# The first inner tile of two up projections computed by plain products, with the pair sums of the late token tile behind it

## The chip, the cores and the metric

The kernel runs on 1 core of one Trainium2 chip. The metric is the device time of a run in microseconds (us): the median of 3 runs before the change is 2680.4 us (2679.09 to 2680.55).

## What is computed

One inference step of a decoder trunk of two layers: an S5 layer with a GLU, a ConvFFN, the projection to keys and values, attention, and a second ConvFFN. It handles 1024 prompt tokens and 64 sample tokens of width 1024. The change touches the up projection of the ConvFFN (`w_up` is 1024 x 5632, gate and val with 2816 columns each), which runs once in each layer:

```
def conv_ffn(x, buf, w_up, conv_w, conv_b, w_down):
    seq_len = x.shape[1]
    h = x @ w_up
    hp = jnp.concatenate([buf.astype(h.dtype), h], axis=1)
    hc = conv_b + conv_w[0] * hp[:, 0:seq_len]
    for tap in range(1, CONV_W):
        hc = hc + conv_w[tap] * hp[:, tap:tap + seq_len]
    gate, val = jnp.split(hc, 2, axis=-1)
    out = (jax.nn.gelu(gate) * val) @ w_down
    return out, hp[:, -(CONV_W - 1):]

x = x + rmsnorm(a_out, post_g)                       # the layer's mixer or attention
x = x + rmsnorm(conv_ffn(rmsnorm(x, f_pre_g), ...))  # twice: layer 0 and layer 1
```

## The kernel before

**Three products for one.** Every operand is split into a high part in the matmul's format and a low part with the rest (`split_evac`: ACT casts the high part in line 144, DVE subtracts for the low part in line 145). A product is three matmuls, hi·hi, lo·hi and hi·lo (`mm3`, lines 809 to 811).

**Tokens.** The normed tokens stand transposed in `xT_hi` and `xT_lo`, 128 to a tile: prompt tiles 0 to 7 and the 64 sample tokens (NTT). The matrix product before (GLU output in layer 0, `o_proj` in layer 1) ends token tile by token tile in the order NTT, 0, 3, 1, 4, 2, 5, 6, 7; the first five are called EARLY. Each goes through a queue (`Tail`): square sum on ACT (824), post norm and residual sum on DVE (854), square sum, second norm on DVE (864), then at `pop` the transposes on PE (870) and the split into `xT`. What stands last in the queue when the up projection begins is popped between its first products.

**Seven products for eight.** An inner tile f is 128 gate and 128 val columns, 22 tiles in all. For the first 768 tokens the kernel does not form the 8 block products (2 halves of the inner axis 1024, 2 token groups of 384, gate and val) but 7, in the manner of Strassen and Winograd. That needs sums on both sides. On the token side `Combos.pair` (905 to 919) is called for token tiles 3, 4 and 5, each paired with 0, 1, 2: t1 = yb_a - ya_a (911), t3 (912), t2 (913), t4 (914), a and b being the halves of a token row. t1 and yb_b go into `xT`, t2 to t4 into 8 tiles of their own. On the weight side `inputs(f)` loads the raw gate and val tiles (512 KB each, two buffers), forms s1 to s4 on DVE (1109 to 1112, 128x512 each) and splits 4 weight tiles of 128x1024 (whi on ACT, wlo on DVE). `first(f)` runs the 7 products, 12 matmuls of 384 columns each, 84 in all; `rest(f, s)` runs 24 matmuls of 320 columns for the other tokens; `conv` and `outputs` follow on ACT, DVE and POOL and end in a store to the scratch tensor `gd`, from which the down projection loads its pieces (gr<-gd).

**The start.** Tile 0 runs its first product and copies it (1146), then pops token 5 with its pair sums, then 6, then 7, then the rest.

**What sets the order.** The program text gives the dependences; a scheduler with a model of the timeline lays out each engine's queue, so that an edit at one place can change the order elsewhere. Each engine, and SP, which issues the DMAs, works its queue in order.

Of the kernel before, what the change touches and what calls it, by code (L numbers as in the profile page):

```python
# [12 lines left out]
F32R = mybir.dt.float32r  # L13
I32 = mybir.dt.int32
AF = mybir.ActivationFunctionType
ALU = mybir.AluOpType
# [21 lines left out]
NF = FF // P  # L38
# [35 lines left out]
def trunk_kernel(ctx, tc, I, O):  # L74
    nc = tc.nc
    V = nc.vector
    A = nc.scalar
# [4 lines left out]
    def nm(s):  # L82
        uid[0] += 1
        return f"{s}_{uid[0]}"
# [6 lines left out]
    def psum(tag="mm"):  # L91
        return pspool.tile([P, 512], F32, tag=tag, name=nm(tag), bufs=5 if tag == "mm" else 3)
# [48 lines left out]
    def split_evac(hi_ap, lo_ap, ps_ap, scale=None):  # L141

        if scale is None:
            A.copy(hi_ap, ps_ap)  # L144
            V.tensor_tensor(lo_ap, ps_ap, hi_ap.bitcast(F32), ALU.subtract)  # L145
        else:
            A.mul(hi_ap, ps_ap, scale)
            V.scalar_tensor_tensor(lo_ap, ps_ap, scale, hi_ap.bitcast(F32), op0=ALU.mult, op1=ALU.subtract)
# [608 lines left out]
    EARLY, LATE = ORDER_O[:5], ORDER_O[5:]  # L757
# [108 lines left out]
    def transposed(y, n):  # L866
        ps = psum_t()
        m = y.shape[1] // P
        for c in range(m):
            PE.transpose(ps[:, c * n : (c + 1) * n], y[:, c * P : (c + 1) * P], ident[0:n, 0:n])  # L870
        return ps[:, 0 : m * n].rearrange("p (c t) -> p c t", c=m)

    def tail_b(y, tt, scale=None):

        t0, n = tokens(tt)
        for h in range(2):
            split_evac(xh[:, 4 * h : 4 * h + 4, t0 : t0 + n], xl[:, 4 * h : 4 * h + 4, t0 : t0 + n],
                       transposed(y[:, 512 * h : 512 * h + 512], n), scale)
# [4 lines left out]
    HT = 384  # L883

    class Combos:
        def __init__(self):
            self.tiles = [slot("acc", [P, 3, HT], F32R) for _ in range(8)]
# [5 lines left out]
        def rhs(self, s, kt):  # L893

            return [self.view(s, part, kt)[:, 0] for part in range(2)]
# [8 lines left out]

        def pair(self, ya, yb, tt):

            t0 = tt * P
            tr = lambda y: transposed(y, P)
            t1, t2, t3, t4 = [slot("gr") for _ in range(4)]
            a, b = slice(0, 512), slice(512, D)  # L910
            V.tensor_tensor(t1, yb[:, a], ya[:, a], ALU.subtract)
            V.tensor_tensor(t3, yb[:, b], yb[:, a], ALU.subtract)
            V.tensor_tensor(t2, yb[:, b], t1, ALU.subtract)
            V.tensor_tensor(t4, ya[:, b], t2, ALU.subtract)
            split_evac(xh[:, 0:4, t0 : t0 + P], xl[:, 0:4, t0 : t0 + P], tr(t1))
            split_evac(xh[:, 4:8, t0 : t0 + P], xl[:, 4:8, t0 : t0 + P], tr(yb[:, b]))
            for s, t in enumerate((t2, t3, t4)):
                self.store(s, tr(t), t0 - HT)

    class Tail:  # L920
# [1 line left out]


        def __init__(self):
            self.n, self.q, self.combos, self.gain, self.lag = [], [], None, None, 2

        def add(self, y, tt, *a, aside=False, **kw):
            tail_a(y, tt, *a, aside=aside, **kw)
# [11 lines left out]
        def pop(self):  # L940
            if self.q:
                y, tt = self.q.pop(0)
                if self.combos and HT <= tt * P < 2 * HT:
                    self.combos.pair(self.first, y, tt)
                else:
                    tail_b(y, tt)
                    self.first = y

    tail = Tail()

# [139 lines left out]
    def ffn_up(i, down):  # L1090
# [3 lines left out]
        u3 = lambda t: t.rearrange("p (k f) -> p k f", f=P)  # L1094

        st, cvos = {}, {}
        cb = tail.combos

        def inputs(f):
            raws, hbs = [], []  # L1100
            for s in range(2):
                raw = pools["w"].tile([P, 1024], F32, tag="raw", name=nm("raw"), bufs=2)
                rv = u3(raw)
                nc.sync.dma_start(rv, wv[:, :, s * FF + f * P : s * FF + (f + 1) * P])
                raws.append(rv)
            a11, a12, a21, a22 = [r[:, 4 * k : 4 * k + 4] for r in raws for k in range(2)]
            s12, s34 = u3(slot("xr")), u3(slot("xr"))
            s1, s2, s3, s4 = [t[:, 4 * k : 4 * k + 4] for t in (s12, s34) for k in range(2)]
            V.tensor_tensor(s1, a21, a22, ALU.add)
            V.tensor_tensor(s2, s1, a11, ALU.subtract)  # L1110
            V.tensor_tensor(s3, a11, a21, ALU.subtract)
            V.tensor_tensor(s4, a12, s2, ALU.subtract)
            ws = []
            for r in (raws[0], s12, s34, raws[1]):
                hi, lo = u3(wslot("whi", F32R)), u3(wslot("wlo", F32R))
                split_evac(hi, lo, r)
                ws.append((hi, lo))
# [17 lines left out]
        NAHEAD = 1  # L1135

        def first(f):


            (wg, w12, w34, wv_), (hg, hv), _ = st[f]  # L1140
            lo, hi = slice(2, 2 + HT), slice(2 + HT, 2 + 2 * HT)
            p1, p2, p3 = psum(), psum(), psum()
            v1, v2, v3 = [t[:, 0:HT] for t in (p1, p2, p3)]
            m1, u2, u3_ = hv[:, lo], hg[:, hi], hv[:, hi]
            prod(p1, wg, 0, x(0, 0), True)
            A.copy(m1, v1)  # L1146
            if f < NAHEAD:
                prod(p1, wg, 4, x(4, 0), False)
                A.copy(hg[:, lo], v1)
                yield  # L1150
# [6 lines left out]
            if f >= NAHEAD:  # L1157
                prod(p1, wg, 4, x(4, 0), False)
                A.copy(hg[:, lo], v1)
# [58 lines left out]


        inputs(0)  # L1220
        g = first(0)
        for _ in range(3):
            next(g)
            tail.pop()
        while tail.q:
            tail.pop()
        for s in range(2):
            rest(0, s)
            conv(0, s)
        outputs(0)  # L1230
        for f in range(NAHEAD, NF):
# [819 lines left out]
    first = {}  # L2051
# [52 lines left out]
```

## Time and profile before

| | us |
|---|---|
| median of 3 runs | 2680.4 |
| the profiled run's own time | 2684.83 |
| its span, first to last instruction | 2682.9 |
| PE busy / DVE busy / ACT busy in the span | 2500.6 / 1963.5 / 1270.9 |
| the up projection of layer 0 begins | 436.2 |
| the up projection of layer 1 begins | 1908 |

The mean granted clock of PE is 0.976. PE is TensorE, DVE is VectorE, ACT is ScalarE, POOL is GpSimd; PEld are PE's weight loads. A timeline line gives the start, the length, the engine, the line of the kernel, the operation, out<-in, the shape, and in brackets how long the engine had been idle and what ended it. Matmul records are longer than their pitch, since they overlap; the distance between two starts is what one costs.

### The profile page before, as it was taken

To read this page: it belongs to the slowest core of one execution; us is meant where nothing else is said; L and a number is where in the kernel's file an instruction comes from. 1 tells how busy PE (TensorE), PEld (TensorE's weight loads), DVE (VectorE), ACT (ScalarE), POOL (GpSimd) and SP (SyncE) were. 2 spreads that over 40 slices of the span, in tenths; PEclk is the share of its full clock that TensorE was granted. 3 is DMA by queue.
4 is the path that set the end of the run, shared out by engine and by line. 5 is a ranking of instruction groups with operands and counts; after the bars stand their busy time and mean duration, and the time that the engine had idled before them with its cause. 6 is when DMAs were issued, how large, how long until landed. Compare 5 with 4: busy or idle time off the path is not lost.

```text
span 2682.9 us, 39622 instructions
## 1 busy us (share of the span) xinstructions
PE 2500.6 (93%) x14234; PEld 2203.5 (82%) x14234; DVE 1963.5 (73%) x3683; ACT 1270.9 (47%) x2559; POOL 657.3 (24%) x1062
## 2 busy tenths in 40 slices
PE   3778998999999989999999899989799999998997
PEld 2777887999999967778777788877699999996775
DVE  7994358777777789984232688875877777778999
ACT  6763334444444454354322677764544444444432
POOL 3220030111111175501201222113011111137661
PEclk9999998999999999999999899999899999999998
DMA  5443233222222233444646433335322222233334
GB/s 145 99 98 88 85 124 124 65 83 74 74 74 74 89 116 92 127 145 166 204 157 211 104 79 95 97 105 171 115 69 79 74 74 74 74 104 107 94 102 145
DMA packets 265688, 286.77 MB, mean 107 GB/s; under 512 B 42268, under 2 KB 212564, under 8 KB 265492
## 3 DMA queue, kind: packets, MB, share of 16 engines
q1 hardware_dynamic: 261892, 273.55, 33.0%
q0 software_dynamic: 3088, 9.77, 1.7%
q8 instruction: 113, 1.85, 0.3%
q10 hardware_dynamic: 512, 0.92, 0.1%
q14 instruction: 83, 0.68, 0.1%
HBM read 193.58 MB, written 70.93 MB: 99 GB/s over the span
## 4 chain that ended last, share of the span: by engine, by line
PE 58%; DVE 13%; DMA 4%; issue 3%; ACT 3%; POOL 2%; SPq 0%; DVEq 0%; POOLq 0%; ACTq 0%
PE mm L809 17%; PE mm L810 17%; PE mm L811 17%; DVE acc L1428 2%; DMA gr<-gd 1%; DVE xT_lo L145 1%; DVE S L1898 1%; PE mm L1417 1%; ACT S L1902 1%; DVE wst L145 1%; DVE xT_hi L145 1%; DVE acc L854 1%; PE mm L1436 1%; PE tr L870 1%; PE mm L1926 1%
## 5 line engine op out<-in xcount | busy, mean ns | idle before, releaser
L809 PE MATMUL mm<-xT_hi,whi 128*128 128x384 f32 (+1 forms) x1408 | 457.0, 325 | 2.0 <-ACT acc L1146 1.8
L810 PE MATMUL mm<-xT_lo,whi 128*128 128x384 f32 (+1 forms) x1408 | 456.3, 324 | 1.6 <-DVE xT_lo L145 1.6
L811 PE MATMUL mm<-xT_hi,wlo 128*128 128x384 f32 (+1 forms) x1408 | 454.2, 324 | 0.0
L809 PEld LDWEIGHTS mm<-xT_hi,whi 128*128 128x128 f32 x1408 | 265.4, 189 | 3.8 <-ACT acc L1146 2.4
L810 PEld LDWEIGHTS mm<-xT_lo,whi 128*128 128x128 f32 x1408 | 265.7, 189 | 2.4 <-DVE xT_lo L145 2.3
L811 PEld LDWEIGHTS mm<-xT_hi,wlo 128*128 128x128 f32 x1408 | 265.4, 189 | 0.8
L1195 POOL COPY cvo<-acc 128x2 f32<-128x2 f32 x88 | 53.3, 606 | 818.5 <-ACT acc L1178 818.5
L809 PE MATMUL mm<-whi,xT_hi 128*128 128x512 f32 x608 | 243.9, 404 | 4.9 <-ACT whi L792 4.7
L1192 DVE SCALAR_TENSOR_TENSOR acc<-acc,cpar,acc 128x1104 f32<-128x1104 f32 x176 | 240.0, 1385 | 4.7 <-ACT acc L1190 4.6
L810 PE MATMUL mm<-wlo,xT_hi 128*128 128x512 f32 x608 | 241.9, 398 | 0.1
L811 PE MATMUL mm<-whi,xT_lo 128*128 128x512 f32 x608 | 241.7, 399 | 0.0
L144 ACT CAST whi<-raw 128x1024 fp32r<-128x1024 f32 x88 | 92.5, 1051 | 253.5 <-PE mm L811 245.2
L1428 DVE TENSOR_TENSOR acc<-mm,acc 128x512 f32<-128x512 f32 x279 | 184.7, 680 | 9.8 <-PE mm L811 9.3
L145 DVE TENSOR_TENSOR wlo<-raw,whi 128x1024 fp32r<-128x1024 f32 x88 | 107.7, 1224 | 107.0 <-PE mm L810 91.6
L809 PE MATMUL mm<-acc,whi 128*128 128x384 f32 x528 | 179.1, 339 | 0.0
L811 PE MATMUL mm<-acc,wlo 128*128 128x384 f32 x528 | 178.7, 339 | 0.0
L810 PE MATMUL mm<-acc,whi 128*128 128x384 f32 x528 | 178.3, 338 | 0.0
L809 PEld LDWEIGHTS mm<-whi,xT_hi 128*128 128x128 f32 x608 | 115.6, 191 | 36.2 <-ACT whi L792 5.6
L810 PEld LDWEIGHTS mm<-wlo,xT_hi 128*128 128x128 f32 x608 | 114.7, 189 | 27.8 <-DVE wlo L793 0.8
L811 PEld LDWEIGHTS mm<-whi,xT_lo 128*128 128x128 f32 x608 | 114.4, 188 | 27.6 <-issue 0.8
L1190 ACT ACTIVATE acc<-acc,cpar 128x1104 f32<-128x1104 f32 x88 | 114.1, 1311 | 18.1 <-DVE acc L1161 11.9
L145 DVE TENSOR_TENSOR wlo<-xr,whi 128x1024 fp32r<-128x1024 f32 x88 | 107.6, 1223 | 16.7 <-ACT whi L144 8.6
(572 smaller groups left out, 6255.9 us busy)
## 6 DMA issues: line engine op xcount, KB each, us to landing
raw<-in_w_up_dram SPq DMA_DIRECT2D x88, 512.0 KB
gd<-acc SPq DMA_DIRECT2D x44, 552.0 KB
raw<-in_w_down_dram SPq DMA_DIRECT2D x44, 512.0 KB
gr<-gd SPq DMA_DIRECT2D x80, 256.0 KB
raw<-in_glu_w_dram SPq DMA_DIRECT2D x40, 256.0 KB
acc<-in_cache_k_dram SPq DMA_DIRECT2D x16, 512.0 KB
acc<-in_cache_v_dram SPq DMA_DIRECT2D x16, 512.0 KB
xj<-in_x_prompt_dram SPq DMA_DIRECT2D x8, 512.0 KB
```

What stands on the lines that cost most here:

```text
L144: A.copy(hi_ap, ps_ap)
L145: V.tensor_tensor(lo_ap, ps_ap, hi_ap.bitcast(F32), ALU.subtract)
L809: PE.matmul(out, lh, rh, start=start, stop=False, **kw)
L810: PE.matmul(out, lh, rl, start=False, stop=False, **kw)
L811: PE.matmul(out, ll, rh, start=False, stop=stop, **kw)
L854: V.scalar_tensor_tensor(y[:, hs], y[:, hs], r[0:n], xr[0:n, hs], op0=ALU.mult, op1=ALU.add)
L870: PE.transpose(ps[:, c * n : (c + 1) * n], y[:, c * P : (c + 1) * P], ident[0:n, 0:n])
L1190: A.activation(hc, hb[:, 2 : 2 + TG], AF.Identity, bias=cp[:, ft, 3:4], scale=cp[:, ft, 2:3])
L1192: V.scalar_tensor_tensor(hc, hb[:, tap : tap + TG], cp[:, ft, tap : tap + 1], hc, op0=ALU.mult, op1=ALU.add)
L1195: GP.tensor_copy(co[:, 0:2], hb[:, SEQ : SEQ + 2])
L1417: PE.matmul(pa[h], lt, wt[:, h * 512 : (h + 1) * 512], start=st and j == 0, stop=sp and j == len(seq) - 1)
L1428: V.tensor_tensor(a, ps, a, ALU.add)
```

## The change

For tile 0 `plain()` takes the place of `first(0)`: the 8 block products from the raw weights and from what `xT` holds (tokens 0 to 2, and t1 and yb_b of tokens 3 to 5), 96 matmuls, in the order gate and val on tokens 0 to 2, then gate and val on tokens 3 to 5. With it s1 to s4 and two of the four splits of tile 0 go away. The evacuation is 4 copies on ACT and 2 sums on DVE where it was 2 copies and 5 sums. `pair` becomes a generator: t1 and yb_b first; t2, t3 and t4 at `tail.end()`, which runs at once for EARLY tokens and behind `plain()` for token 5.

```diff
         def pair(self, ya, yb, tt):
...
-            t1, t2, t3, t4 = [slot("gr") for _ in range(4)]
             a, b = slice(0, 512), slice(512, D)
+            t1 = slot("gr")
             V.tensor_tensor(t1, yb[:, a], ya[:, a], ALU.subtract)
-            V.tensor_tensor(t3, yb[:, b], yb[:, a], ALU.subtract)
-            V.tensor_tensor(t2, yb[:, b], t1, ALU.subtract)
-            V.tensor_tensor(t4, ya[:, b], t2, ALU.subtract)
             split_evac(xh[:, 0:4, t0 : t0 + P], xl[:, 0:4, t0 : t0 + P], tr(t1))
             split_evac(xh[:, 4:8, t0 : t0 + P], xl[:, 4:8, t0 : t0 + P], tr(yb[:, b]))
+            yield
+            t2, t3, t4 = [slot("gr") for _ in range(3)]
+            V.tensor_tensor(t2, yb[:, b], t1, ALU.subtract)
+            V.tensor_tensor(t3, yb[:, b], yb[:, a], ALU.subtract)
+            V.tensor_tensor(t4, ya[:, b], t2, ALU.subtract)
             for s, t in enumerate((t2, t3, t4)):
                 self.store(s, tr(t), t0 - HT)
...
-                    self.combos.pair(self.first, y, tt)
+                    g = self.combos.pair(self.first, y, tt)
+                    next(g)
+                    self.left.append(g)
+                    if tt in EARLY:
+                        self.end()
...
+        def end(self):
+
+            while self.left:
+                next(self.left.pop(), None)
...
+            ops = [raws[0], None, None, raws[1]]
+            if f:
...
+                s12, s34 = ops[1:3] = u3(slot("xr")), u3(slot("xr"))
...
+            for j, r in enumerate(ops):
+                if r is not None:
+                    ws[j] = u3(wslot("whi", F32R)), u3(wslot("wlo", F32R))
+                    split_evac(*ws[j], r)
...
+        def plain():
+
+
+            ws, hbs, _ = st[0]
+            lo, hi = slice(2, 2 + HT), slice(2 + HT, 2 + 2 * HT)
+            for s in range(2):
+                ps, hb, w = psum(), hbs[s], ws[3 * s]
+                v = ps[:, 0:HT]
+                prod(ps, w, 0, x(0, 0), True)
+                A.copy(hb[:, hi], v)
+                prod(ps, w, 4, x(4, 0), False)
+                A.copy(hb[:, lo], v)
+                yield
+            for s in range(2):
+                ps, hb, w = psum(), hbs[s], ws[3 * s]
+                prod(ps, w, 0, x(0, HT), True)
+                prod(ps, w, 4, x(4, HT), False)
+                V.tensor_tensor(hb[:, hi], ps[:, 0:HT], hb[:, hi], ALU.add)
+                yield
...
-        g = first(0)
-        for _ in range(3):
-            next(g)
-            tail.pop()
+        for k, _ in enumerate(plain()):
+            if k < 2 or len(tail.q) > 3 - k:
+                tail.pop()
         while tail.q:
             tail.pop()
+        tail.end()
```

The order changes at three places. First DVE's queue at the start of layer 0, around t1 of token 5 (`gr<-acc_4006,acc_3956`, line 911 before, 912 now). `raw_4230` and `raw_4232` are tile 0's weights, `raw_4501` and `raw_4503` tile 1's; `acc_4136` is token 7, `acc_4071` token 6. Before:

```order
L854 SCALAR_TENSOR_TENSOR acc_4136<-acc_4136,rr_4175,xr_4167 128x1024
L864 SCALAR_TENSOR_TENSOR acc_4071<-acc_4071,rr_4191,acc_2343 128x1024
L1111 TENSOR_TENSOR xr_4235<-raw_4230,raw_4232 128x512
L1112 TENSOR_TENSOR xr_4235<-raw_4230,xr_4234 128x512
L911 TENSOR_TENSOR gr_4291<-acc_4006,acc_3956 128x512
L912 TENSOR_TENSOR gr_4293<-acc_4006 128x512
L120 TENSOR_SCALAR rv_4218<-ss_4216 128x1
L913 TENSOR_TENSOR gr_4292<-acc_4006,gr_4291 128x512
```

Now:

```order
L854 SCALAR_TENSOR_TENSOR acc_4136<-acc_4136,rr_4175,xr_4167 128x1024
L134 SCALAR_TENSOR_TENSOR rr_4191<-rs_4190,rr_4191 128x1
L145 TENSOR_TENSOR wlo_4516<-xr_4505,whi_4515 128x1024
L1125 TENSOR_TENSOR xr_4506<-raw_4501,raw_4503 128x512
L912 TENSOR_TENSOR gr_4275<-acc_4006,acc_3956 128x512
L130 SCALAR_TENSOR_TENSOR rs_4190<-rr_4191,rv_4189 128x1
L1126 TENSOR_TENSOR xr_4506<-raw_4501,xr_4505 128x512
L120 TENSOR_SCALAR rv_4218<-ss_4216 128x1
L917 TENSOR_TENSOR gr_4398<-acc_4006,gr_4275 128x512
L918 TENSOR_TENSOR gr_4399<-acc_4006 128x512
```

The weight work ahead of t1 is now tile 1's, and token 6's norm (864) has moved behind t1 and the other pair sums.

Second ACT's queue at the start of layer 1, around token 2's square sum over 1024 columns (`acc_18506` before, `acc_18504` now; line 824). `raw_18819` is the second weight tile of inner tile 0, `raw_19037` and `raw_19039` are those of inner tile 1. Before:

```order
L144 CAST whi_18839<-raw_18819 128x1024
L144 CAST acc_17913<-tr_18405 128x128
L824 ACTIVATE gr_18600,ss_18601<-acc_18506 128x1024
L824 ACTIVATE gr_18645,ss_18646<-acc_18615 128x512
L144 CAST acc_17914<-tr_18405 128x3x128
```

Now:

```order
L144 CAST whi_19047<-raw_19037 128x1024
L144 CAST acc_17912<-tr_18403 128x3x128
L2050 COPY acc_18689<-mm_18691 128x512
L144 CAST whi_19059<-raw_19039 128x1024
L824 ACTIVATE gr_18598,ss_18599<-acc_18504 128x1024
L824 ACTIVATE gr_18643,ss_18644<-acc_18613 128x512
```

Tile 1's two casts now stand ahead of that square sum; before, they stood some 20 rows behind it.

Third ACT's queue where layer 0's up projection passes into the down projection. `acc_8664` (now `acc_8662`) is the gate of the last inner tile at its gelu (1198, now 1223). `gr_8786` (now `gr_8784`) is the piece of the down projection's fifth token step, `gr_8814` (now `gr_8812`) that of the sixth; `raw_8840` (now `raw_8838`) belongs to the down projection's next weights. Before:

```order
L144 CAST xT_hi<-raw_8840 128x512 x2
L1422 COPY acc_8762<-mm_8763 128x512
L1198 ACTIVATE acc_8664<-acc_8664 128x1104
L144 CAST xT_hi<-xr_8843 128x512
L1422 COPY acc_8762<-mm_8764 128x512
L144 CAST xT_hi<-xr_8844 128x512
L1212 COPY gr_8724<-tr_8719 18x512
L1422 COPY acc_8790<-mm_8791 128x512
L144 CAST xT_hi<-xr_8844 128x512
L1422 COPY acc_8790<-mm_8792 128x512
L144 CAST xT_lo<-gr_8786 128x2x128
L144 CAST xT_lo<-gr_8814 128x2x128
```

Now, first the row of the fifth step and, further on, the gelu:

```order
L1237 COPY gr_8722<-tr_8717 18x512
L144 CAST xT_lo<-gr_8784 128x2x128
L144 CAST wst_8777<-xr_8747 128x512
L144 CAST xT_lo<-xr_8756 128x2x128
L144 CAST wst_8781<-raw_8744 128x512
L144 CAST wst_8805<-raw_8744 128x512
L1215 ACTIVATE acc_8662<-acc_8527,cpar_2673 128x1104
```

```order
L144 CAST xT_hi<-xr_8841 128x512
L144 CAST xT_hi<-raw_8838 128x512 x2
L1223 ACTIVATE acc_8662<-acc_8662 128x1104
L144 CAST xT_lo<-gr_8812 128x2x128
L1447 COPY acc_8788<-mm_8790 128x512
```

The fifth step's cast has moved ahead of the last tile's conv and gelu; the sixth step's stands directly behind the gelu.

More of the change, by code (lines that the diff above doesn't have):

```diff
@@ L924, in __init__ @@
         def __init__(self):
-            self.n, self.q, self.combos, self.gain, self.lag = [], [], None, None, 2
+            self.n, self.q, self.left, self.combos, self.gain, self.lag = [], [], [], None, None, 2
         def add(self, y, tt, *a, aside=False, **kw):
@@ L1099, in inputs @@
         def inputs(f):
-            raws, hbs = [], []
+            raws, hbs, ws = [], [], [None] * 4
             for s in range(2):
@@ L1105, in inputs @@
                 raws.append(rv)
[L1106 to L1117, printed above, removed]
+            ops = [raws[0], None, None, raws[1]]
+            if f:
+                a11, a12, a21, a22 = [r[:, 4 * k : 4 * k + 4] for r in raws for k in range(2)]
+                s12, s34 = ops[1:3] = u3(slot("xr")), u3(slot("xr"))
+                s1, s2, s3, s4 = [t[:, 4 * k : 4 * k + 4] for t in (s12, s34) for k in range(2)]
+                V.tensor_tensor(s1, a21, a22, ALU.add)
+                V.tensor_tensor(s2, s1, a11, ALU.subtract)
+                V.tensor_tensor(s3, a11, a21, ALU.subtract)
+                V.tensor_tensor(s4, a12, s2, ALU.subtract)
+            for j, r in enumerate(ops):
+                if r is not None:
+                    ws[j] = u3(wslot("whi", F32R)), u3(wslot("wlo", F32R))
+                    split_evac(*ws[j], r)
             for s in range(2):
@@ L1133, in x @@
             return lambda k: (xh[:, k0 + k, t0 : t0 + HT], xl[:, k0 + k, t0 : t0 + HT])
-        NAHEAD = 1
+        def plain():
[15 more added lines that the diff above has]
+                yield
         def first(f):
@@ L1146, in first @@
             A.copy(m1, v1)
[L1147 to L1150, printed above, removed]
             prod(p2, w12, 4, lambda k: cb.rhs(0, k), True)
@@ L1156, in first @@
             V.tensor_tensor(u3_, v3, u3_, ALU.add)
-            if f >= NAHEAD:
-                prod(p1, wg, 4, x(4, 0), False)
-                A.copy(hg[:, lo], v1)
+            prod(p1, wg, 4, x(4, 0), False)
+            A.copy(hg[:, lo], v1)
             prod(p3, w34, 4, x(4, HT), False)
@@ L1230, in ffn_up @@
         outputs(0)
-        for f in range(NAHEAD, NF):
+        for f in range(1, NF):
             inputs(f)
```

## The prediction

> **What bounds the kernel now.** I read the page's busy line first, then busy time and granted clock by stretches around the two up projections.
>
> ```profile
> PE 2500.6 (93%) x14234; PEld 2203.5 (82%) x14234; DVE 1963.5 (73%) x3683; ACT 1270.9 (47%) x2559; POOL 657.3 (24%) x1062
> ...
> 439.00:449.00 10.00, 0.27 (x2) 0.16 (x2) 9.96 (x27) 4.19 (x6) 0.22 (x1) 0.73 0.27 109
> 449.00:457.00 8.00, 6.86 (x25) 6.36 (x26) 7.59 (x15) 3.08 (x6) 0.31 (x2) 0.50 0.43 127
> 475.00:925.00 450.00, 450.00 (x2752) 448.24 (x2751) 331.86 (x370) 199.51 (x282) 53.60 (x169) 1.00 0.24 76
> 1898.00:1906.00 8.00, 1.18 (x6) 0.69 (x5) 8.00 (x35) 4.14 (x10) 0.24 (x2) 0.69 0.76 262
> 1923.00:1931.00 8.00, 3.16 (x15) 2.87 (x14) 7.12 (x15) 4.80 (x8) 0.00 (x0) 0.84 0.01 2
> 1950.00:2400.00 450.00, 450.00 (x2753) 448.24 (x2753) 330.59 (x368) 198.15 (x279) 81.92 (x163) 1.00 0.24 77
> ```
>
> A row of a stretch gives its length, then busy time of PE, PEld, DVE, ACT and POOL, the granted clock, the DMA share and GB/s. From 475 to 925 us and from 1950 to 2400 us PE never idles, at full clock. So whatever is won or lost where an up projection starts goes straight into the time, and DVE's 73% over the whole span says nothing about that place. In 439–449 PE works 0.27 of 10 us while DVE works 9.96: DVE is the bound of that stretch, and in 1898–1906 again (8.00 of 8).
>
> **Place 1, the start in layer 0.** PE's timeline, then DVE's and ACT's (start, length, what ended the idle time before).
>
> ```profile
> 434.94 1.04 PE L870 MATMUL tr<-ident,acc 128*128 128x128 f32 x8
> ...
> 437.23 0.33 PE L811 MATMUL mm<-xT_hi,wlo 128*128 128x384 f32 x1
> ...
> 438.80 0.34 PE L811 MATMUL mm<-xT_hi,wlo 128*128 128x384 f32 x1
> 448.87 1.09 PE L870 MATMUL tr<-ident,gr 128*128 128x128 f32 x4 [9.73 <-DVE gr L911]
> ...
> 452.81 0.69 PE L809 MATMUL mm<-xT_hi,whi 128*128 128x384 f32 x1 [1.14 <-ACT acc L1146]
> ```
>
> ```profile
> 442.86 1.23 DVE L145 TENSOR_TENSOR wlo<-xr,whi 128x1024 fp32r<-128x1024 f32 x1
> ...
> 445.64 1.28 DVE L864 SCALAR_TENSOR_TENSOR acc<-acc,rr,acc 128x1024 f32<-128x1024 f32 x1
> ...
> 448.04 0.69 DVE L911 TENSOR_TENSOR gr<-acc,acc 128x512 f32<-128x512 f32 x1
> 448.64 0.69 DVE L912 TENSOR_TENSOR gr<-acc 128x512 f32<-128x512 f32 x1
> ```
>
> ```profile
> 451.33 1.04 ACT L144 CAST whi<-raw 128x1024 fp32r<-128x1024 f32 x1 [0.75 <-DMA raw<-in_w_up_dram]
> 452.29 0.47 ACT L1146 COPY acc<-mm 128x384 f32<-128x384 f32 x1
> 452.65 0.59 ACT L144 CAST xT_hi<-tr 128x512 fp32r<-128x512 f32 x1
> ```
>
> PE runs the first product of 12 matmuls and then has nothing until t1 of token 5 (L911) comes off DVE: 9.73 us. From 437.23 to 438.80 are nine steps, so a matmul of 384 columns costs 0.174 us at full clock.
>
> The added work: the first tile takes 8 products instead of 7, 12 more matmuls, 12 x 0.174 = 2.1 us in each layer. Nothing covers them; they stand on the engine that bounds the tiles.
>
> The wait: ahead of token 5's transposes PE now has about 36 matmuls, not 12 (both gate products on tokens 0 to 2 and the first of val). That is 24 x 0.174 = 4.2 us more, to about 443.1. When does t1 come? A 512-wide DVE operation costs 0.60 (448.64 less 448.04), a 1024-wide norm 1.28, a wlo 1.23. Ahead of t1 four sums, one wlo and token 6's norm go away: 2.4 + 1.23 + 1.28 = 4.9. But the new order pulls the weights of tile 1 into the hole: two wlo and three sums, 4.3. So t1 comes only about 0.6 us earlier, near 448.0. Less weight preparation in tile 0 hardly makes t1 earlier; the gap gets shorter because PE has more to do meanwhile.
>
> On ACT stand behind that: a whi of tile 1 that needs the DVE sum after t1 (448.6 + 1.04), two xT_hi of token 5 (0.59 each), and only then the copy (0.47) for which PE's next product waits. PE goes on at about 451.3. Before, it went on at 452.81 with 12 of 84 matmuls and 12 of 20 transposes behind it; now at 451.3 with 36 of 96 and 8 of 20. That is 1.5 us earlier, 12 matmuls less to go (2.1, the added ones counted) and 4 transposes more (half of 1.04, 0.5): **-3.1 us**. Bounds: 0, if DVE slips by two more wlo and a sum (3.1); -5.2, if the clock stays up (12 x 0.174 at half rate are 2.1 more). t2 to t4 (three sums, 1.8 us of DVE, and 12 transposes) move behind the plain products. Tile 1 is the first to read them, after some 60 matmuls or 10 us, and that covers them; without this cover they would cost their 1.8.
>
> The gap shrinks from 9.73 to about 5 us (443.1 to 448). In 449–457, behind 9.73 us of idleness, the clock is 0.50; in 1923–1931, which holds a gap of 4.84, it is 0.84 on the mean. So 5 us may well cost the clock, and I leave that loss in the sum.
>
> [...]
>
> **Place 2, the start in layer 1.**
>
> ```profile
> 1905.81 1.94 PE L870 MATMUL tr<-ident,acc 128*128 128x128 f32 x8 [6.82 <-DVE acc L864]
> ...
> 1928.38 1.92 PE L870 MATMUL tr<-ident,acc 128*128 128x128 f32 x8 [4.84 <-DVE acc L864]
> ...
> 1897.78 1.06 ACT L824 ACTIVATE gr<-acc 128x1024 bf16<-128x1024 f32 x1 [1.00 <-DVE acc L854]
> 1922.80 1.05 ACT L144 CAST whi<-raw 128x1024 fp32r<-128x1024 f32 x1 [3.19 <-DMA raw<-in_w_up_dram]
> 1917.18 1.01 SPq L1104 DMA_DIRECT2D raw<-in_w_up_dram  x2
> ```
>
> Here PE waits for the norms of token 2 (6.82) and token 6 (4.84), not for token 5's pair. The second wait goes: two groups of 24 matmuls more stand ahead of token 6's transposes, and DVE no longer sits behind the whi that waited for tile 1's weights (ACT, 1922.80). That removes 4.84 and half rate over the 8 transposes (1.92 less 1.04, 0.9).
>
> Against it: on DVE a wlo more stands ahead of token 2's norm (1.23), and on ACT both casts of tile 1's raw weights stand ahead of token 2's square sum (1897.78 here). Such a load takes 5.6 us to the cast (1917.18 to 1922.80); issued when its buffer comes free, near 1897, it holds token 2's chain until 1902 or 1903, up to 5 us. Behind the square sum, DVE was fully busy in 1898–1906, partly with work that is not of this chain and can be done during the wait. So the first stall grows by 1.2 at least and 5 at most; I take 2.6, nearer the small end because of that work. With the 2.1 of added matmuls: -4.84 - 0.9 + 2.6 + 2.1 = **-1.0 us** (bounds -2.4 and +1.4).
>
> **Place 3, from up to down, once in each layer.** The diff touches nothing there, but the scheduler's order changes.
>
> ```profile
> 952.29 1.22 PE L1417 MATMUL mm<-whi,xT_lo 128*128 128x512 f32 x2 [3.69 <-ACT xT_lo L144]
> 957.83 1.20 PE L1417 MATMUL mm<-whi,xT_lo 128*128 128x512 f32 x4 [1.90 <-DVE xT_lo L145]
> ...
> 951.84 0.71 ACT L144 CAST xT_lo<-gr 128x256 fp32r<-128x256 f32 x2
> ...
> 2419.70 1.04 PE L1417 MATMUL mm<-whi,xT_lo 128*128 128x512 f32 x2 [3.40 <-ACT xT_lo L144]
> ```
>
> PE loses 3.69 + 1.90 us: the fifth token step of the down projection waits for a cast that stands on ACT behind the last gelu (L1198). In the new order this cast stands ahead of the gelu, so a step's 12 matmuls (512/384 x 0.174 = 0.23 each) can run before the wait, 2.8 us; the sixth step still waits behind the gelu, whose own products now come later on PE. Bounds for each: -5.6, both waits gone; +5.6, one load of 5.6 us more in the chain, because the next weights (raw, L1284) now stand on SP behind several gr<-gd loads. I take half of the 2.8, **-1.5 us each, -3 together**.
>
> **Sum.** -3.1 - 1.0 - 3 = -7.1 us. The profiled run took 2684.83, so 2677.7 in its place; it lies 4.4 above the median of the runs, 2680.4, so I expect a median of about **2673 us**.
>
> **Rivals.**
> 1. *Tile 1's preparation takes the place of tile 0's.* For it speaks the order, which gives t1 back only 0.6 us. With place 2 at its +1.4 and nothing at place 3, -3.1 + 1.4 = -1.7; with place 1 at 0 as well, +1.4: 2679 to 2682, say 2680. Against it: PE's 4.2 us of more work at place 1 do not depend on DVE.
> 2. *The down projection's next weights come late*, and the kernel is slower. SP works in order, and those two loads now follow gr<-gd loads whose buffers PE frees. ACT's cast of them stands ahead of the gelu and so ahead of the sixth step; each us that they land after ACT comes to them is lost on PE, in both layers. Instead of -1.5 each this gives no change from +2.0 each (-3.1 - 1.0 against it) and 5.4 us slower from +4.8 each; at the load's full 5.6 in each layer, -4.1 + 11.2 = +7.1: 2687.5. Against it: PE frees those buffers early in the down projection.
> 3. *The clock stays up* at place 1 (-2.1) and place 3 shrinks by all of the 2.8 or more: -3.1 - 2.1 - 1.0 and -2.8 to -5.6 twice: -11.8 to -17.4: 2663 to 2669, say 2666.
> 4. *The order inside the tiles* also changes, but costs nothing: PE is 450.00 of 450.00 busy there and DVE 332.
>
> **Chances.** Forecast, -5.4 to -12 (2668 to 2675): 0.50. Rival 1: 0.24. Rival 2: 0.13. Rival 3: 0.13. About 0.2%, 5.4 us, is what a measurement of this kernel can tell from no change. So faster 0.63 (forecast and rival 3), same 0.24, slower 0.13. The range for 8 in 10 takes in rival 1 with the bounds of place 2 and half of rival 3, and leaves rival 2 out: 2663 to 2683.
>
> **What would show it.** Place 1: a gap of about 5 us where 9.73 was, still ended by t1 off DVE at nearly the same time, then a wait for ACT's copy. Place 2: a first stall of 8 to 10 us where 6.82 was, and none for token 6. Place 3: the first wait at the sixth step, and shorter. Rival 2 would show as ACT waiting for raw<-in_w_down ahead of the last gelu. I am wrong if t1 comes several us earlier or later, or if PE idles between 475 and 925.

## The result and the profile after

The changed kernel takes 2698.1 us (median of 4 runs, 2696.38 to 2701.99) beside 2680.4 before: a ratio of 1.0066 with a 95% interval of 1.0051 to 1.0082. It is **slower by 17.7 us**, where 2673 was forecast. The profiled execution took 2697.7 us; its span is 13.0 us longer than that of before, whose profiled run lay 4.4 above its own median. The 13.0 can be followed through the traces.

The busy line of the page after:

```profile
span 2695.9 us, 39558 instructions
PE 2504.3 (93%) x14258; PEld 2200.9 (82%) x14258; DVE 1952.6 (72%) x3665; ACT 1276.7 (47%) x2559; POOL 725.7 (27%) x1062
```

PE is busy for 93% as before, and DVE a little less. The line shows nothing of the loss. A table of where PE stands does: for the same matmul in both traces, the time in before, and how much later it comes after the change.

| PE's instruction | before, us | after |
|---|---|---|
| first product of the up projection, layer 0 | 436.2 | -1.7 |
| first token step of the down projection, layer 0 | 942.7 | +1.8 |
| end of that down projection | 1207.2 | +6.1 |
| end of the products with k and v | 1471.0 | +2.8 |
| last product with w_q in the last head of attention | 1732.5 | +2.8 |
| last product of that head's weights with v | 1764.4 | +7.1 |
| end of o_proj | 1898.1 | +9.7 |
| last token step ahead of down, layer 1 | 2410.2 | +8.5 |
| end of the down projection, layer 1 | 2666.8 | +12.7 |

**The gaps at the two starts came out much as said.** PE's timeline after the change, at place 1, place 2 and place 3 in layer 0 (start, length, and in brackets the idle time and what ended it):

```profile
436.20 0.69 PE L810 MATMUL mm<-xT_lo,whi 128*128 128x384 f32 x1 [1.09 <-DVE xT_lo L145]
436.68 0.53 PE L811 MATMUL mm<-xT_hi,wlo 128*128 128x384 f32 x1
...
439.24 0.50 PE L810 MATMUL mm<-xT_lo,whi 128*128 128x384 f32 x1
...
447.99 1.09 PE L870 MATMUL tr<-ident,gr 128*128 128x128 f32 x4 [4.07 <-DVE rs L130]
...
450.19 1.56 PE L809 MATMUL mm<-xT_hi,whi 128*128 128x384 f32 x3 [0.26 <-ACT xT_hi L144]
...
942.97 0.50 PE L1442 MATMUL mm<-whi,gr 128*128 128x512 f32 x1 [0.47 <-DVE acc L1186]
...
946.83 0.50 PE L1442 MATMUL mm<-whi,xT_lo 128*128 128x512 f32 x1 [0.80 <-ACT acc L1447]
...
960.95 2.07 PE L1442 MATMUL mm<-whi,xT_lo 128*128 128x512 f32 x4 [4.74 <-DVE xT_lo L145]
...
1916.67 1.94 PE L870 MATMUL tr<-ident,acc 128*128 128x128 f32 x8 [8.03 <-DVE rr L123]
...
1928.26 0.45 PE L809 MATMUL mm<-xT_hi,whi 128*128 128x384 f32 x1 [0.77 <-ACT acc L1157]
```

The gap at place 1 is 4.07 us where 9.73 was, PE goes on at 450.19, the stall at place 2 is 8.03, and token 6's wait is gone. At place 3 one wait of 4.74 stands where 3.69 and 1.90 were, but two waits are new there, 0.47 and 0.80.

**The loss is in the stretches that were taken for granted.** Busy time by stretches inside the tiles, after:

```profile
480.00:920.00 440.00, 438.78 (x2668) 433.38 (x2667) 312.41 (x355) 193.23 (x269) 101.72 (x160) 1.00 0.23 75
1960.00:2400.00 440.00, 438.89 (x2668) 433.34 (x2667) 311.22 (x354) 191.60 (x267) 100.23 (x160) 1.00 0.24 76
```

and before:

```profile
480.00:920.00 440.00, 440.00 (x2689) 438.24 (x2688) 323.53 (x362) 194.57 (x275) 50.23 (x165) 1.00 0.24 76
1960.00:2400.00 440.00, 440.00 (x2692) 438.24 (x2691) 323.73 (x361) 195.06 (x274) 81.81 (x163) 1.00 0.24 76
```

PE reads as 99.7% busy, yet it starts 21 to 24 matmuls fewer in 440 us. At 0.147 to 0.174 us each that is 3 to 4 us of work. Records overlap: one of 384 columns is 0.34 us long at a pitch of 0.174, so the first 0.17 us of every hole hide in the busy time; the number in brackets and the weight loads (PEld, -4.9) show it.

For the comparisons below I use **lost time**: the time from the last matmul of the product before, less PE's work at full pitch (0.174 us per matmul of 384 columns, 0.147 per 320, 0.2325 per 512, 0.109 per transpose, all distances of starts in these traces). The plain products' 2.1 us in a layer are work and come on top. "Start" is the first 25 us of work, "tiles" up to 467, "down" from 520 to 690 (the passage, place 3, lies between). The last column is how long DVE's 128x1024 difference of two softmax rows takes in the last head.

| kernel | start 0 | tiles 0 | down 0 | start 1 | tiles 1 | down 1 | DVE op |
|---|---|---|---|---|---|---|---|
| before | 15.9 | 0.8 | 4.3 | 20.0 | 0.8 | 6.9 | 1.28 |
| **after** | 13.0 | **4.5** | **10.3** | 11.5 | **4.2** | **12.7** | **3.31** |
| e1 ring kept | 9.9 | 0.9 | 4.8 | 14.7 | 0.6 | 7.4 | 3.31 |
| e7, the same kernel | 9.4 | 1.1 | 4.6 | 15.4 | 0.6 | 7.8 | 3.31 |
| e2 pair alone | 13.8 | 1.0 | 4.1 | 24.6 | 1.1 | 6.1 | 1.28 |
| e3 plain alone | 9.2 | 7.7 | 9.2 | 13.0 | 9.6 | 13.0 | 3.32 |
| e4 layer 1 alone | 15.7 | 1.0 | 4.3 | 11.5 | 6.5 | 11.0 | 1.28 |
| e5 layer 1, slots | 13.8 | 1.1 | 4.1 | 12.9 | 0.9 | 7.7 | 1.28 |
| e6 both, slots | 10.1 | 5.7 | 11.7 | 12.1 | 0.6 | 7.0 | 3.31 |
| e8 sums kept | 10.5 | 0.9 | 5.0 | 12.8 | 1.2 | 7.3 | 3.31 |
| e9 = e8, halves | 12.1 | 1.1 | 4.8 | 13.2 | 0.9 | 7.2 | 2.21 |
| e10 = after, halves | 10.2 | 4.6 | 10.2 | 13.3 | 5.6 | 12.6 | 2.21 |
| e11 = e8, on DVE | 10.6 | 1.0 | 5.9 | 15.5 | 1.2 | 9.3 | 1.28 |

e1 and e7 are two profiles of one kernel: they differ by 0.8 at most. Starts differ by more between kernels that share their code there, up to 3 us. A row is one execution: those of e4 and e8, for example, took 2682.4 and 2676.3 us, 7.1 and 4.8 below the medians of their runs. The edge at 520 lies among the waits of place 3, so "down" moves by up to 2 us with it; with the edge at 525, behind those waits, down loses 2.9 and 5.5 before (layer 0, layer 1) and 8.0 and 9.9 after.

**Why the tiles lose.** In the last ten of a layer's 22 tiles PE's order after the change runs the rest products (320 columns) of gate and val in groups of 42, where before most come in groups of 24 or fewer. What engines wait for between 480 and 920 us (total us, times, longest), after:

```profile
DVE wlo L145 <- PE mm L810: 109.9, 19, 6.2
...
PEld mm L809 <- DVE acc L1186: 3.6, 9, 0.5
```

and before:

```profile
DVE wlo L145 <- PE mm L810: 42.8, 21, 5.3
DVE acc L1164 <- PE mm L811: 31.7, 14, 2.3
DVE acc L1155 <- PE mm L811: 23.6, 18, 2.4
```

Before, DVE's adds that empty PSUM wait for PE. After, PE waits for one of them (L1186, `V.tensor_tensor(u2, v3, u2, ALU.add)`). One of the nine places, on DVE and on PE:

```profile
742.31 1.23 DVE L145 TENSOR_TENSOR wlo<-raw,whi 128x1024 fp32r<-128x1024 f32 x1 [5.98 <-PE mm L810]
743.45 0.55 DVE L1186 TENSOR_TENSOR acc<-mm,acc 128x384 f32<-128x384 f32 x1
```

```profile
743.52 0.34 PE L811 MATMUL mm<-acc,wlo 128*128 128x384 f32 x1
744.06 0.41 PE L809 MATMUL mm<-xT_hi,whi 128*128 128x320 f32 x1 [0.20 <-DVE acc L1186]
```

DVE has nothing to do for 5.98 us: its next operation is the split of a later tile's raw weights, whose buffer PE must free first. Only when that split (1.23) is over comes the add, and the rest group that needs the emptied PSUM waits for it: 0.54 us from start to start where 0.17 is the pitch. In the layer's earlier tiles the same add stands behind the same split, but more of PE's work stands ahead of the next rest group, and the add ends 0.4 to 5.0 us before that group starts. With the one wait for POOL that the trace lists, 3.6 + 0.6 us in layer 0, against 3.7 more of lost time; in layer 1 it is 4.1 + 0.2 against 3.4.

**Down** shows the same kind. The weight loads' waits for the adding copy of a token step, in down 0 after, then before:

```profile
PEld mm L809 <- DVE acc L1453: 11.2, 10, 2.6
```

```profile
PEld mm L809 <- DVE acc L1428: 6.2, 11, 1.4
```

5.0 more, where down 0 loses 6.0 more by the table and 5.1 more with the edge at 525. In down 1 the same row reads 18.2 after and 12.7 before.

**The last head of attention** loses 4.3 us (2.8 to 7.1 in the first table) though the diff is nowhere near. DVE, then POOL, then PE there, after:

```profile
1745.95 3.31 DVE L1937 SCALAR_TENSOR_TENSOR S<-S,cc,S 128x1024 f32<-128x1024 f32 x1
...
1755.64 2.89 DVE L1937 SCALAR_TENSOR_TENSOR S<-S,cc,S 128x896 f32<-128x896 f32 x1
...
1759.28 0.47 DVE L148 SCALAR_TENSOR_TENSOR xT_lo<-tr,sgc,xT_hi 128x256 fp32r<-128x256 f32 x1
```

```profile
1745.75 2.43 POOL L1895 TENSOR_TENSOR kh<-qraw,kh 128x1024 fp32r<-128x1024 f32 x1 [5.07 <-ACT kh L1894]
1755.20 2.39 POOL L1895 TENSOR_TENSOR kl<-qraw,kl 128x1024 fp32r<-128x1024 f32 x1 [7.02 <-ACT kl L1894]
```

```profile
1759.90 0.63 PE L1945 MATMUL tr<-ident,S 128*128 128x128 f32 x4 [2.85 <-DVE xT_lo L148]
1760.36 1.75 PE L1951 MATMUL mm<-v,wt 128*128 128x128 f32 x8
```

and DVE and POOL before:

```profile
1743.19 1.28 DVE L1912 SCALAR_TENSOR_TENSOR S<-S,cc,S 128x1024 f32<-128x1024 f32 x1
...
1751.29 1.14 DVE L1912 SCALAR_TENSOR_TENSOR S<-S,cc,S 128x896 f32<-128x896 f32 x1
```

```profile
1743.52 3.20 POOL L1870 TENSOR_TENSOR kh<-qraw,kh 128x1024 fp32r<-128x1024 f32 x1 [5.59 <-ACT kh L1869]
1751.87 2.81 POOL L1870 TENSOR_TENSOR kl<-qraw,kl 128x1024 fp32r<-128x1024 f32 x1 [5.14 <-ACT kl L1869]
```

The same DVE operation takes 3.31 us in place of 1.28 where a split of w_o on POOL has started 0.2 us ahead of it, and 2.89 in place of 1.14 the second time: it does its work when POOL has finished (1748.18 and 1757.59). Before, DVE's operation started 0.33 and 0.58 us ahead of POOL's, and it was POOL that took longer (3.20 and 2.81 for 2.4). PE waits 2.85 us behind it (0.17 before), and then runs at half rate for some 3 us (1.75 for eight matmuls that take 1.16 before at full rate).

The order is not what changed here: from 1700 to 1757 us before the change, and at the same places after it, the rows of PE, DVE, ACT and POOL follow each other in the same order. What differs is when the w_o tile is there for ACT's cast, which POOL's split follows. Before, then after:

```profile
1742.40 1.05 ACT L1869 CAST kh<-qraw 128x1024 fp32r<-128x1024 f32 x1 [0.43 <-DMA qraw<-in_w_o_dram]
```

```profile
1744.60 1.07 ACT L1894 CAST kh<-qraw 128x1024 fp32r<-128x1024 f32 x1
```

The load's last packet ends 4.08 us after its issue before and 3.33 after. In the four kernels with seven products in layer 0 (before, e2, e4, e5) it is 4.03 to 4.12, and a 16 KB packet of the instruction queue (q8) starts 0.07 to 0.56 us behind the issue; in the other nine it is 3.26 to 3.37, and that packet starts 0.33 to 0.78 us ahead of it. So an instruction load that falls beside the w_o load is the likely reason; no run moves it alone.

### The profile page after: what moved, and what is told of

Read it like the earlier page. It is cut to its first block, busy times and chain, and to the rows that moved or that the text cites. A ratio compares the mean times of both kernels' runs of the same rounds, so it can differ in the third digit from the quotient of the medians.

```text
span 2695.9 us, 39558 instructions
## 1 busy us (share of the span) xinstructions
PE 2504.3 (93%) x14258; PEld 2200.9 (82%) x14258; DVE 1952.6 (72%) x3665; ACT 1276.7 (47%) x2559; POOL 725.7 (27%) x1062
## 4 chain that ended last, share of the span: by engine, by line
PE 55%; DVE 15%; DMA 5%; ACT 3%; POOL 3%; issue 3%; SPq 0%; DVEq 0%; POOLq 0%; ACTq 0%
PE mm L809 17%; PE mm L810 16%; PE mm L811 16%; DVE acc L1453 2%; DVE xT_lo L145 2%; DMA gr<-gd 1%; DVE S L1923 1%; ACT S L1927 1%; POOL xr L1323 1%; DVE acc L854 1%; DMA raw<-in_w_down_dram 1%; DVE wst L145 1%; DVE xT_hi L145 1%; PE mm L1951 1%; DVE S L1937 1%
## 5 line engine op out<-in xcount | busy, mean ns | idle before, releaser
L809 PE MATMUL mm<-xT_hi,whi 128*128 128x320 f32 (+1 forms) x1440 | 470.9, 329 | 3.5 <-DVE acc L1186 2.0
L810 PE MATMUL mm<-xT_lo,whi 128*128 128x384 f32 (+1 forms) x1440 | 468.0, 325 | 1.1 <-DVE xT_lo L145 1.1
L811 PE MATMUL mm<-xT_hi,wlo 128*128 128x384 f32 (+1 forms) x1440 | 465.1, 324 | 0.0
L1220 POOL COPY cvo<-acc 128x2 f32<-128x2 f32 x88 | 151.9, 1726 | 676.1 <-ACT acc L1203 676.1
L809 PEld LDWEIGHTS mm<-xT_hi,whi 128*128 128x128 f32 x1440 | 271.7, 189 | 12.3 <-DVE acc L1186 8.3
L810 PEld LDWEIGHTS mm<-xT_lo,whi 128*128 128x128 f32 x1440 | 272.3, 189 | 1.8 <-DVE xT_lo L145 1.8
L811 PEld LDWEIGHTS mm<-xT_hi,wlo 128*128 128x128 f32 x1440 | 272.1, 189 | 0.2
L810 PE MATMUL mm<-acc,whi 128*128 128x384 f32 x504 | 170.6, 338 | 0.0
L811 PE MATMUL mm<-acc,wlo 128*128 128x384 f32 x504 | 170.1, 338 | 0.0
L809 PE MATMUL mm<-acc,whi 128*128 128x384 f32 x504 | 170.0, 339 | 0.0
L1215 ACT ACTIVATE acc<-acc,cpar 128x1104 f32<-128x1104 f32 x88 | 115.5, 1314 | 28.6 <-DVE acc L1186 18.9
L1923 DVE CUSTOM_DVE_ANT_0 S<-mm,tb 128x512 f32<-128x512 f32 (+3 forms) x192 | 101.4, 552 | 22.7 <-PE mm L1921 19.2
```

Source lines behind the costliest of these rows:

```text
L809: PE.matmul(out, lh, rh, start=start, stop=False, **kw)
L810: PE.matmul(out, lh, rl, start=False, stop=False, **kw)
L811: PE.matmul(out, ll, rh, start=False, stop=stop, **kw)
L1215: A.activation(hc, hb[:, 2 : 2 + TG], AF.Identity, bias=cp[:, ft, 3:4], scale=cp[:, ft, 2:3])
L1220: GP.tensor_copy(co[:, 0:2], hb[:, SEQ : SEQ + 2])
L1923: V.tensor_tensor_reduce(S_[j][:, k0 : k0 + w], ps[:, 0:w], H["tb"][:, b0 : b0 + w], 0.125, -3e38, ALU.add, ALU.max, mx[:, j, c : c + 1])
```

## The experiments

All edits are against the changed kernel unless said otherwise; ratios are against the kernel before on the same chip.

**e1 and e7: the ring of weight buffers kept in step.** Weight tiles go round 11 buffers. Tile 0 now splits two operands, not four, so every later tile gets other buffers, four of them free earlier. Here tile 0 takes the buffers of the two missing operands without filling them. No instruction is added.

```diff
             for j, r in enumerate(ops):
+                if r is None:
+                    wslot("whi", F32R), wslot("wlo", F32R)
                 if r is not None:
```

> The changed kernel, but tile 0 also takes the four weight buffers that it no longer fills (no instruction is added; the ring of 11 buffers just goes on as before the change). Theory A, run-ahead: with four buffers fewer taken, the weights of tile 1 and all later ones are laid out earlier, and that drives the order inside the tiles and in the down projection into a worse one; then the tiles' loss (3.9 + 3.5 us by my sum of PE work) and the down projection's (5.4 + 4.4) go, the gains at the two starts (1.3 + 6.4) stay: 2670 to 2676. Theory B, the late pair sums and the added products cost the time themselves: 2694 to 2700. Theory C, the down projection loses for a reason of its own: 2680 to 2686.

> The kernel of e1_ring once more, for a second profile and a narrower interval. If the 8 us lost between the last head of attention and o_proj come from the order there (64 rows of PE differ from before), they come again, and the ratio to before is 0.999 to 1.002. If they were chance, it is 0.996 to 0.998.

Measured 2683.0 us (1.0008, 0.9994 to 1.0021) and again 2681.1 (1.0003, 0.9993 to 1.0012). The time lies in the range of theory C and not of A, but what A says of the stretches holds: the losses in the tiles and in down are gone in both layers, and no weight load waits for an add in the tiles. Busy time there, in e7:

```profile
480.00:920.00 440.00, 440.00 (x2689) 438.20 (x2688) 323.60 (x362) 193.57 (x273) 48.45 (x161) 1.00 0.24 77
1960.00:2400.00 440.00, 440.00 (x2690) 438.24 (x2690) 322.22 (x360) 194.18 (x273) 81.67 (x161) 1.00 0.24 77
```

So it is not the plain products that slow the tiles, but the order in which the scheduler lays out all that follows when the ring is out of step. That the kernel is still no faster than before comes from attention and o_proj: 6.5 us ahead at 1732, 2.2 at 1764, 0.3 at 1898 (e7). The 4.3 in the last head come again, as e7's text expected, but not from PE's order, which in attention's last stretch, from 1690 on, is that of before up to 1776.

**e2: the new order of the pair sums alone**, with the seven products of tile 0 as before.

> The pair as in the changed kernel (t1 and yb_b first, then t2, t3, t4, at once), but tile 0 by the seven products as before. A: no buffer is saved, so no loss in the tiles: 2677 to 2683. B (the sums' new order hurts): above 2688.

```diff
-            if f:
+            if True:
...
-        for k, _ in enumerate(plain()):
...
+        g = first(0)
+        for _ in range(3):
+            next(g)
+            tail.pop()
+            tail.end()
```

2687.0 us, 1.0019 (1.0006 to 1.0031), between the two ranges. Tiles, down and attention are as before; start 1 is 4.6 us worse (24.6). Why, I did not follow up.

**e3: the plain products alone**, the old `pair` in one piece.

> Plain products in tile 0, but the pair whole and in its old order (t1, t3, t2, t4 at once). A: the buffers are still saved, the tiles and the down projection still lose: 2693 to 2701. B (late t2 to t4 are at fault): 2675 to 2684.

```diff
+            t1, t2, t3, t4 = [slot("gr") for _ in range(4)]
...
-            t1 = slot("gr")
...
-            yield
-            t2, t3, t4 = [slot("gr") for _ in range(3)]
```

2707.5 us, 1.0094 (1.0067 to 1.0122): the worst of all and 6.5 us above the range of A, with 7.7 and 9.6 in the tiles. The late pair sums are not what hurts. The groups of 42 begin earlier here (15 of them in a layer, not 10), and PE's waits for the add follow: 5.5 us in 13 places and 2.1 for POOL, together 7.6, beside 7.7 lost.

**e4: the change in layer 1 only.**

> The change in layer 1 alone; layer 0 as before (with the pair's new order). By my sum layer 1 wins 6.4 at its start net of the added products and loses 3.5 in the tiles, 0.9 at the passage and 4.4 in the down projection: +2.4, and attention, which stands ahead of it, is not touched: 2680 to 2686. If attention's 3.5 us came with the change in layer 0, they are absent here; if they come back, they have another cause.

```diff
-            if f:
+            if f or not (i == 1):
...
+        if i == 1:
             for k, _ in enumerate(plain()):
...
+        else:
+            g = first(0)
```

2689.4 us, 1.0028 (1.0013 to 1.0042), 3.4 us above the range. Layer 0 and attention are as before, and layer 1 has the gain at its start (11.5) and the losses (6.5 and 11.0). Each layer's loss is made by its own tile 0; attention's goes with layer 0.

**e5: layer 1 only, and four buffers of the ring passed over ahead of tile 0's own**; **e6: the same in both layers.**

> The change in layer 1 alone (layer 0 as before, with the pair's new order), and tile 0 of layer 1 takes four weight buffers that it does not fill, ahead of its own. In the built program the tiles of both layers keep groups of 24 matmuls on the other tokens, as before the change, and attention keeps its order. Theory A (the order inside the tiles and in the down projection carries the loss): layer 1 keeps its gain at the start, 5 to 7 us, and loses nothing in tiles and down: a ratio to before of 0.9970 to 0.9985. Theory B (the change itself slows the tiles): as e4_layer1, 1.0015 to 1.0040.

> Both layers changed, four buffers taken in each, but ahead of tile 0's own, so that 7 and not 3 of the 11 are free when tile 1's weights are prepared. In the built program layer 0 has the groups of 42 as in the changed kernel, layer 1 those of 24. If the order is what costs: layer 0 loses 3 to 5 us in the tiles and 4 to 6 in the down projection, layer 1 under 1 in each; against e1_ring 7 to 11 us more. If the ring's position is what costs: as e1_ring.

```diff
+            for _ in range(0 if f else (0, 4)[i]):
+                wslot("whi", F32R)
             for j, r in enumerate(ops):
```

(On top of e4's edits in e5; in e6 the pair is `(4, 4)`.) e5: 2675.3 us, 0.9985 (0.9976 to 0.9994), faster than both kernels. e6: 2684.5, 1.0021 (1.0012 to 1.0031). In e6 the same four buffers do different things: layer 1 comes back to groups of 24 and to 0.6 and 7.0, layer 0 stays with 42 and with 5.7 and 11.7. So it is not the number of buffers but the order that comes out. In time e6 is by the ratios only 3.5 and 4.8 us above e1 and e7, not 7 to 11: by its trace layer 0 ends 12 us later than in e1, but o_proj loses 4.2 us in e1 and gains 1.1 in e6, which the expectation had not counted. e6's waits in the tiles, layer 0 (layer 1 has none):

```profile
PEld mm L809 <- DVE acc L1188: 3.6, 9, 0.5
PEld tr L1237 <- POOL cvo L1223: 1.9, 2, 1.4
```

Over all thirteen traces and both layers: groups of 42, with the add late for PE and 4.2 us or more lost in the tiles, go together eight times; without such groups no more than 1.2 is lost, eighteen times. Down goes with them: 9.2 to 13.0 in the eight, 4.1 to 7.8 in the others, but for e11's 9.3. With down's edge at 525 the two sets part in each layer: 6.8 to 9.8 against 2.9 to 4.1 in layer 0, 8.5 to 10.4 against 4.3 to 7.3 in layer 1.

**e8: plain products, but tile 0 still forms s1 to s4 and splits all four operands.**

> Plain products in both layers, but tile 0 still forms its four sums and splits all four weight tiles, which nothing reads. If the start is shorter because DVE has less to do, the gain there goes (13 to 16 us lost in layer 0's start, as before the change); if it is shorter because PE has more that can run, it stays within 2 us of e1_ring (about 10 in layer 0, 15 in layer 1). Tiles with groups of 24: under 1 us lost in them.

```diff
-            if f:
+            if True:
```

2681.1 us, 1.0013 (1.0002 to 1.0024). Tiles and down as in e1, start 0 as short (10.5): the work that the change takes from tile 0's DVE and ACT is not what shortens the start. It is 10.8 us ahead of before at 1732 and loses 4.3 of it by 1757.

**e9, e10, e11: the stall in the last head.** The w_o split on POOL in two halves, in e8's kernel (e9) and in the changed kernel itself (e10); three of the four splits on DVE, in e8's kernel (e11).

```diff
-                (GP if k2 < OWG else V).tensor_tensor(lo, raw, hi.bitcast(F32), ALU.subtract)
+                for j in range(2):
+                    (GP if k2 < OWG else V).tensor_tensor(lo[:, j], raw[:, j], hi.bitcast(F32)[:, j], ALU.subtract)
```

```diff
-            OWG = 4
+            OWG = 1
```

> The kernel of e8 with one edit in attention: POOL's split of a w_o tile (128x1024, 2.4 us) is issued as two of 128x512. Theory (DVE and POOL exclude each other there, so that DVE's 128x1024 difference of two softmax rows takes 3.31 us where it took 1.28, and the 128x896 one 2.89 where it took 1.14): DVE can get in between the halves, so those two fall to at most 2.5 and 2.1 us, PE's wait of 2.85 us for xT_lo behind them to at most 1.7, and the 4.3 us that e8 loses between 1730 and 1755 to 2 or less; the time is 2 to 4 us below e8's 2681.1, ratio 0.998 to 0.9995. Rival (the order of PE's own rows in the last head costs the 4.3): nothing changes, ratio 1.0013 as e8.

> The changed kernel itself with the same edit alone (the w_o splits on POOL in halves). Theory: the loss at the end of attention (+2.8 to +7.1 us against before between 1735 and 1764) shrinks from 4.3 to 2 or less, the losses in the tiles (3.7 and 3.4) and in the two down projections (6.0 and 5.8) stay; 2 to 4 us below the changed kernel's ratio of 1.0066, so 1.005 to 1.006. Rival (the PE order there costs it): 1.0066 with 4.3 in that stretch.

> The kernel of e8 with three of the four w_o splits on DVE in place of POOL. Theory: without a POOL operation beside them the two DVE differences take 1.28 and 1.14 us again. DVE carries 3 x 1.2 us more in a stretch in which it was 4.9 of 5 us busy, so what is gained there (up to 4.3) may be given back: 0 to 4 us below e8, ratio 0.998 to 1.0015. Rival (the stretch of 3.31 is DVE's own, for example of its operands): they stay at 3.31 and 2.89.

DVE's two operations in e9, then in e11:

```profile
1735.27 2.21 DVE L1938 SCALAR_TENSOR_TENSOR S<-S,cc,S 128x1024 f32<-128x1024 f32 x1
...
1743.86 1.84 DVE L1938 SCALAR_TENSOR_TENSOR S<-S,cc,S 128x896 f32<-128x896 f32 x1
```

```profile
1742.61 1.28 DVE L1937 SCALAR_TENSOR_TENSOR S<-S,cc,S 128x1024 f32<-128x1024 f32 x1
1748.78 1.15 DVE L1937 SCALAR_TENSOR_TENSOR S<-S,cc,S 128x896 f32<-128x896 f32 x1
```

With halves DVE gets in after one of them; without POOL the operation has its own length again. PE's wait behind them is 1.43 us in e9 and 1.51 in e10, and the clock stays at 1.00. The stretch costs 0.6 us in e9 (7.9 ahead at 1732, 7.3 at 1757) and 0.7 in e10, where 4.3 stood; in e11 2.4. e9 takes 2678.1 us (0.999, 0.9979 to 1.0), e10 2694.0 (1.0048, 1.0036 to 1.006), e11 2677.7 (0.9982, 0.9974 to 0.9991). All three came out as the theory said, e10 a little better. In e10 the tiles and down lose what they lost after the change, so that the causes are separate. e5 and e11 beat both kernels, by 0.15% and 0.18%, which is below what I said a measurement of this kernel can tell; their intervals leave 1 out.

## Why the prediction was wrong

**What failed is rival 4**, the clause that the order inside the tiles also changes, "but costs nothing: PE is 450.00 of 450.00 busy there and DVE 332", and with it the sum's silence on down behind its first steps. The order cost 3.7 and 3.4 us in the tiles and 6.0 and 5.8 in down, 18.9 together, and e1 and e7 take all but about 1 of it back by the ring alone. Two errors lie in it. A full busy row was read as slack for everyone else, though it only says that nobody was late in that order. And DVE's 332 of 450 us was read as room, though DVE works its queue in order (the add at 743.45 us came behind a split that DVE had waited 5.98 us to start): the row to look at was how long it waits for PE with an add behind it (42.8 us in 21 waits before, 109.9 in 19 after). The sentence on what would show me wrong, "if PE idles between 475 and 925", was the right test, and it struck; but busy time shows only 1.2 of the 3.7 us, and the count of matmuls shows them.

**A stretch was not in the sum at all**: attention, 4.3 us in the last head and 2.6 in o_proj, with no line of the diff near it. The 4.3 come from which of DVE and POOL starts first, and not from a new order.

**Place 1** went as described in its gap: 4.07 (about 5), PE went on at 450.19 (451.3), and the clock fell all the same (0.52 in 449 to 457). t1 came at 447.16 in place of 448.04, 0.9 us earlier where 0.6 was forecast, but the whole up projection began 1.7 us earlier; from its start t1 came 0.8 us later (0.7 earlier in e10), so that this agreement is luck. The size is unsure: with the added 2.1 it gave 0.8 us in the profile after, 3.6 in e10, whose start has the same code, against 3.1 forecast. Both have a new wait of 1.09 in the first product; behind it the profile after has half rate (0.32 us between starts from 436.68 to 439.24), and e10's stays at full rate (0.17).

**Place 2** was mis-sized, to the good: -8.5 + 2.1 = -6.4 us, not -1.0. The first stall grew by 1.2, the low bound, and not by 2.6. Token 6's gap cost 6.9 us of lost time, not 4.84 + 0.9, since the clock came back only after the transposes (0.32 us between starts up to 1931.7); and the half rate and the small waits behind the first stall (clock 0.51 in 1906 to 1915) cost 6.1 us before and 3.3 after, 2.8 that I had not counted. In e10, with the same code, the first stall is 9.54, 2.7 longer than before, and place 2 gives -4.6.

**Place 3** went the other way. The step waits once, and later: 4.74 us where 3.69 and 1.90 were, in layer 1 5.32 where 3.40 and 2.43 were, which is 0.8 and 0.5 less. But PE now waits ahead of it as well, for the late add of the last tile (0.47, in layer 1 0.86) and for ACT's copy out of PSUM (0.80 and 0.54). From 467 to 525 us of work the passage lost 0.9 and 1.5 us more than before, where 1.5 less was forecast for each; down behind it lost 5.1 and 4.4 more. Rival 2 did not occur: ACT waits for no load of w_down ahead of the last gelu (at 951.71 in layer 0 after).

So the named places gave -0.8 - 6.4 + 0.9 + 1.5 = -4.8 where -7.1 was forecast, with no term near its size. The rest: tiles +7.1, down +9.5, attention and o_proj +6.9, the earlier start of the up projection -1.7, and 3.3 that come back between down 0 and 1471. Together +13.7, where the spans differ by 13.0. Between 1207 and 1471 every kernel of the study gains 2.0 to 4.1 us on before, whatever its edit; one profile of before stands against them, and I leave their cause open. So stays the reason why the scheduler's choice tips, in layer 0 with seven buffers free and not in layer 1 with the same four passed over: the runs show that it does and what it costs, not by which of its rules. o_proj's 2.6 us were not taken apart.

## What to carry to other kernels

An edit that frees buffers in a scheduled kernel rewrites the order far from it: before pricing the edit, compare the order in every long stretch, and hold the buffers' rotation in place (here by two calls that add no instruction) so that the edit can be measured apart from the reordering. A busy row of 100% is a statement about one order and no reserve; count instructions per stretch, and look for an engine that waits with another's release queued behind it. A win of a few us at one place is smaller than what a reordering can cost, and a shift of half a microsecond can cost as much where two engines exclude each other (here DVE's start against POOL's moved by 0.53 us, and the last head lost 4.3).

## What the runs showed of the hardware

**DVE and POOL exclude each other** on the two operations shown, DVE's difference of two softmax rows and POOL's split of a w_o tile, and the one that starts 0.2 to 0.6 us later waits for the rest of the other: 3.31 us for 1.28, 2.21 with POOL's operation cut in half (e9, e10), 1.28 with none (e11). The traces show it in both directions: before the change it was POOL that waited (3.20 and 2.81 us for 2.4).

**A stall of 2.85 us took the clock.** The stretch behind it, in the last head after the change:

```profile
1761.00:1766.00 5.00, 5.00 (x22) 4.19 (x21) 4.27 (x10) 3.22 (x7) 2.18 (x1) 0.70 0.02 3
```

The granted clock is 0.70 where it was 1.00 in every stretch of that head before, and so a wait that grew by 2.7 us cost 4.3. Waits of 1.43 and 1.51 us at the same place (e9, e10) left it at 1.00. The 2.85 us are the wait alone: from the last matmul of a product ahead of it (start 1756.31) to the first behind it (1760.36) PE ran nothing but transposes for 4.05 us, and no run sets the two lengths apart. Idle time alone does not decide: behind the wait of 1.09 us in the first product of layer 0 the clock fell to half in the profile after (0.32 us between starts), and stayed up in e10's (0.17), which has the same wait.
